# Second half of a projection: natural parts 512 columns wide between transposed parts, with four weight buffers lent by the attention's zone

## The chip, the core and the metric

The kernel runs on one core of one Trainium2 chip. A core has TensorE (matrix products into PSUM), VectorE (DVE), ScalarE (ACT), GpSimd (POOL), and SyncE (SP), whose queue issues the DMAs here. TensorE reads a stationary operand that a weight load (PEld) brings in, and streams a moving operand past it. Each engine executes its own instructions in the order in which the program gives them; semaphores hold one engine until another has finished what it needs.

The metric is the device time of one execution in microseconds. Before the change: median 1905.05 us of three runs (1902.53 to 1905.58).

## The reference

One layer of a streaming encoder. Every token is normalised, multiplied by one combined weight matrix, and its columns feed two branches: differential attention (q, k, v called qa, ka, va) and retention (qb, kb, vb). Each branch is gated (za, zb), projected, merged with two sigmoid gates (ga, gb), projected once more and added to the input.

```python
h = rmsnorm(x, norm_g) @ w_in                    # x: 2048 + 64 tokens x 1024, w_in: 1024 x 6144
qa, ka, va, za, qb, kb, vb, zb, ga, gb = split(h)  # eight parts of 512 columns, then two of 1024
qa, ka = rmsnorm per 64 columns(qa, ka)
a  = softmax(qa1 ka1) - lam * softmax(qa2 ka2)   # 4 heads, block-causal, distance bias
oa = a @ va
ob = retention(qb, kb, vb)                       # 4 heads, running state, blocks of 128 tokens
m  = sigmoid(ga) * ((rmsnorm(oa) * silu(za)) @ w_o_diff) + sigmoid(gb) * ((rmsnorm(ob) * silu(zb)) @ w_o_ret)
y  = x + m @ w_out
```

2048 prompt tokens run as one new stream; 64 sample tokens continue another one with 4096 cached keys and values. The normalised keys, the values and the retention states are outputs too.

## The kernel before

**Precision.** Operands are split into a high and a low part of the fast float format (`wh`, `wl` for weights, `xh`, `xl` for tokens), and each product is three matmuls: high by high, high by low, low by high (L998). A group over the whole inner dimension of 1024 has 8 chunks of 128, hence 24 matmuls.

**A planner orders the program.** The code is a set of Python generators, each a task with a priority. While the program is built, a planner keeps an estimated clock for each engine (`self.pe`, `self.act`, `self.dve`, `self.pool`, `self.dma`), with fixed costs for each instruction (`P`, `A`, `V`, `G`, `ld`, `st`, L204 to L241). A task yields the time or the condition it waits for; the ready task with the lowest priority number goes next (`loop`). Buffers are taken and given back by tag with such times (`take`, `give`). The order in which instructions are emitted is the order in which each engine executes them. The attention has priority 4 and its parts 0 to 3; the projection (`w_stream`) has 9, so it fills what the attention leaves free on TensorE.

**Projection in two halves of 1024 tokens.** The first half also carries the 64 sample tokens in its natural parts, and its transposed parts use a Strassen scheme (`strassen`). The second half does not. Its parts are of two kinds:

- *natural* (`natural`, L1092): 128 tokens are stationary and the weights' columns stream past, so the result has tokens on its partitions. Used for va, ka, qa and vb. With `wide` one 128-token tile makes 512 columns; without it two tiles of 256 columns share one PSUM bank, and the 512 columns of a part come as two calls. In the second half before, all natural parts are of the narrow kind.
- *transposed* (`transposed`, L1288): 128 columns of weights are stationary and tokens stream past in groups of 512, 256 and 320 (the last one with the 64 sample tokens). Used for qb, kb, za, zb, ga, gb in parts of 256 columns.

The second half before runs: va, ka, qa (first 256 columns each), mark `kqv0`; va, ka, qa (last 256 columns each), mark `kqv1`; vb twice; then qb, kb, mark `ret`, za, zb, ga, gb. The marks let the attention's heads 0 and 1, heads 2 and 3, and the retention of this half begin.

**Finishing a group.** PSUM has eight banks by tag: `mm` 2 (projection), `s` 2, `at` 2, `pv` 1, `tp` 1. A va tile leaves through a cast into `thi` (one buffer, L1246), a copy into `ev` (three buffers, L1248) and a difference into `tlo` (two, L1250); each buffer is free when its store to memory is done. ka and qa tiles square, sum, scale, are transposed on `tp` (L1202) and split. Transposed groups leave through `ev` alone (L1307 or L1309, then `put`).

**Weights.** A piece of weights is loaded into staging (`ws`, three buffers, L235 by way of `w_load`), ScalarE casts it into `wh` (L952) and GpSimd computes `wl` (L962). A wide piece is one chunk of 512 columns, a narrow one two chunks of 256; both take two buffers of the tag `w` (12 buffers), so a narrow part takes 8 in all and a wide one 16. In the first half four more, `wx`, stand in the pool of that half's zone. `w_room` (L631) and `w_pair` (L659) choose the buffers. A part keeps its pieces until its last group has read them.

**Attention's zone.** When the first half is over and the tokens of the second are split into high and low parts (`xt_ready`), `attn_zone` (L2676) frees the first half's zone and opens one for the attention: K and V of a head (four buffers each: two of each for a head of the first half, four of each in the second), q (two), and one long score area `row` of 12032 columns (`LATER`), an `Arena` from which contiguous spans are taken and given back piece by piece. For 128 queries and `nk` keys, `qk_block` (L1501) takes two rows of `nk` columns, `softmax` (L1544) exponentiates and combines them, and `at_pv` (L1589) transposes the combined row and multiplies it by V. Retention blocks take two spans of 1024 columns each from the same area, two blocks at a time, beside a table of 1024; its state takes 512.

`h_loader` and `q_loader` load K, V and q. For the very first head `load_head` (L1416) loads K, then q for the first two query pairs, the distance table `dfar`, then V, without a pause. `head_in` (L1464) lets the heads of a half begin 9 us (in the planner's clock) after their mark. When all attention and retention is done, the zone is closed and `out_prep` (L2198) loads the output weights and the first gated operands; `out_stream` begins when `w_stream` is over.

Of the kernel before, what the change touches and what calls it, by code (L numbers as in the profile page):

```python
# [49 lines left out]
LATER = 12032  # L50
# [38 lines left out]

class Arena:  # L90
    def __init__(self, tile, n):
        self.tile = tile
        self.at = [0.0] * (n // GRAIN)
        self.turn = 0

# [9 lines left out]
    def place(self, sizes, now):  # L105
# [18 lines left out]
        return [Span(self.tile[:, a * GRAIN:a * GRAIN + n], a, n) for (a, k, w), n in zip(got, sizes)], t  # L124
# [12 lines left out]
class Hybrid:  # L137
# [71 lines left out]
    def drop(self, span, t, lo=0, hi=None):  # L209
        self.ar.drop(span, t, lo, span.n if hi is None else hi)  # L210

# [419 lines left out]
    def w_room(self, wide, nw, q):  # L631

        if not wide:
            tags, pool, shape = ("w", "w"), self.wp, [128, 2, 256]
        elif nw in (0, 2):
            tags, pool, shape = ("S", "S"), self.ap, [128, 2, 512]
        else:
            tag, pool = yield from self.w_pair()
# [4 lines left out]
        elif u == 0:  # L643
            for tag in tags:
                yield from self.take(tag)
            self.wroom = [self.sb(pool, shape, tag, n, F32R) for tag, n in zip(tags, ("wh", "wl"))]
# [641 lines left out]
    def transposed(self, half, dst, d0, scale=None, grouped=True):  # L1288
        us = []
        groups = [(0, 0, 512), (1, 0, 256), (1, 256, 320)]  # L1290
        for ct in range(2):
            for k, (seg, col, n) in enumerate(groups):
                yield from self.take("mm")
                ps = self.psum("mm")[:, :n]
                last = ct == 1 and k == len(groups) - 1
# [112 lines left out]

    def attn_tables(self):
# [6 lines left out]
    def load_head(self, half, h):  # L1416
# [84 lines left out]
    def qk_block(self, h, p, b, ks, q, pair):  # L1501
# [6 lines left out]
        for c in range(2):  # L1508
            row = yield from self.grab(nk)
# [34 lines left out]
    def softmax(self, st, nk, b, pair):  # L1544
# [4 lines left out]
        half = nk if nk <= 1280 else (nk // 256) * 128  # L1549
# [26 lines left out]
        for sl in parts:  # L1576
# [5 lines left out]
            self.drop(rows[1], t2, sl.start, sl.stop)  # L1582
# [6 lines left out]
    def at_pv(self, h, p, vs, tv, pair, last_pair):  # L1589
# [27 lines left out]
        for kp in range(nkt // 2):  # L1617
# [15 lines left out]
            for row in arows:  # L1633
                self.drop(row, t, 256 * kp, min(256 * kp + 256, row.n))
# [963 lines left out]
    def w_stream(self):  # L2598
# [3 lines left out]
        fva = [(va + 256 * g, lambda half, g=g, f=f: self.natural(half, self.fin_va(g), f))  # L2602
               for g in range(2) for f in (True, False)]
        fva, fva0 = fva[1::2], fva[0]
        fk = [(ka + 256 * g, lambda half, g=g: self.natural(half, self.fin_qk("k", g))) for g in range(2)]
        fq = [(qa + 256 * g, lambda half, g=g: self.natural(half, self.fin_qk("q", g))) for g in range(2)]
        m0, m1 = (None, "kqv0"), (None, "kqv1")
        self.S, self.sunits, self.sraw, self.seg1_read, self.summed = {}, [], [], None, False
# [221 lines left out]
```

## Time and profile before

| quantity | value |
|---|---|
| median of three runs | 1905.05 us |
| the profiled execution, its own time | 1906.88 us |
| its span, first to last instruction | 1904.8 us |
| TensorE busy in the span | 1886.2 us, 99% |
| VectorE, ScalarE, GpSimd busy | 67%, 50%, 31% |
| granted clock, mean | 0.996 |
| second half's W work (natural from 584.0, transposed from 894.0, to the first output matmul) | 584.0 to 1545.5 us |

A matmul's listed duration includes the time it takes to run through the array, and matmuls overlap; the distance from start to start is what one costs when TensorE is full. Rows of busy time by stretches list, after the stretch and its length, busy us (and count) of PE, PEld, DVE, ACT and POOL, then the granted TensorE clock, the DMA engines' busy share and GB/s. Rows in order of time list start, duration, engine, line, operation, destination from source, count, and in brackets the idle time before and what ended it. Rows of waits list total us, times and the longest.

### The profile page before, as it was taken

Reading aid. Unit: us, or ns where it says so; the run is one execution under the profiler, and the core shown is the slowest. Engines: PE = TensorE matmul, PEld = TensorE weight load, DVE = VectorE, ACT = ScalarE, POOL = GpSimd, SP = SyncE. Lnnn points to the kernel's source line nnn. Section 1 sums busy time; section 2 is a strip of 40 time slices with the busy share of each in tenths; the row PEclk is TensorE's granted clock in tenths of the full one; section 3 lists DMA queues with packets and bytes.
Section 4 is the critical chain, followed back from the end, with each engine's and each line's share of the span. In section 5 each row is a group of like instructions: output and inputs, shape, how many; then the busy total and the mean of one; then the engine's idle time right before and its main releaser. Section 6 shows DMA issues by size and latency. Waiting matters only on the chain. (4 is left out here: it accounts for less than half of the span.)

```text
span 1904.8 us, 33589 instructions
## 1 busy us (share of the span) xinstructions
PE 1886.2 (99%) x11690; PEld 1691.2 (89%) x11690; DVE 1277.7 (67%) x3058; ACT 947.4 (50%) x2151; POOL 590.5 (31%) x557
## 2 busy tenths in 40 slices
PE   9999999999998999999999999999999999999999
PEld 7788888888887999999999989999999999999887
DVE  6765766657565787777676765676773139987664
ACT  6434554444443556565555565555565335554221
POOL 2420355556541212221111122111113515522442
PEclk9999999999998999999999999999999999999999
DMA  7654555565557848475325347435216548886542
GB/s 255 215 173 132 161 169 176 168 188 186 175 164 212 241 154 223 144 212 142 99 74 149 99 122 202 110 99 146 80 52 187 173 135 244 257 248 204 173 154 79
DMA packets 361323, 313.10 MB, mean 164 GB/s; under 512 B 67905, under 2 KB 319937, under 8 KB 361154
## 3 DMA queue, kind: packets, MB, share of 16 engines
q1 hardware_dynamic: 361154, 310.97, 55.7%
q8 instruction: 92, 1.51, 0.3%
q14 instruction: 77, 0.63, 0.1%
HBM read 205.43 MB, written 104.60 MB: 163 GB/s over the span
## 5 line engine op out<-in xcount | busy, mean ns | idle before, releaser
L962 POOL TENSOR_TENSOR wl<-ws,wh 128x512 fp32r<-128x512 f32 x125 | 171.9, 1389 | 373.5 <-ACT wh L952 326.1
L998 PE MATMUL mm<-xh,wh 128*128 128x512 f32 (+2 forms) x768 | 255.7, 333 | 0.0
L998 PE MATMUL mm<-xl,wh 128*128 128x512 f32 (+2 forms) x768 | 251.5, 327 | 0.0
L998 PE MATMUL mm<-xh,wl 128*128 128x512 f32 (+2 forms) x768 | 251.4, 327 | 0.0
L998 PE MATMUL mm<-wh,xh 128*128 128x256 f32 (+1 forms) x760 | 249.1, 328 | 0.0
L998 PE MATMUL mm<-wh,xl 128*128 128x256 f32 (+1 forms) x760 | 242.5, 319 | 0.0
L998 PE MATMUL mm<-wl,xh 128*128 128x256 f32 (+1 forms) x760 | 242.1, 319 | 0.0
L1644 DVE TENSOR_TENSOR atl<-at,ath 128x512 fp32r<-128x512 f32 (+1 forms) x144 | 93.6, 660 | 111.5 <-ACT ath L1642 110.9
L998 PEld LDWEIGHTS mm<-xh,wh 128*128 128x128 f32 x768 | 144.9, 189 | 11.1
L998 PEld LDWEIGHTS mm<-xl,wh 128*128 128x128 f32 x768 | 145.1, 189 | 10.7
L998 PEld LDWEIGHTS mm<-wh,xh 128*128 128x128 f32 x760 | 144.5, 190 | 11.2 <-DVE raw L1170 0.2
L998 PEld LDWEIGHTS mm<-wl,xh 128*128 128x128 f32 x760 | 144.5, 190 | 10.9
L998 PEld LDWEIGHTS mm<-xh,wl 128*128 128x128 f32 x768 | 144.8, 189 | 10.5
L998 PEld LDWEIGHTS mm<-wh,xl 128*128 128x128 f32 x760 | 144.3, 190 | 10.7
L1557 ACT ACTIVATE row<-row,a_mx 128x896 f32<-128x896 f32 (+5 forms) x144 | 149.3, 1040 | 8.1 <-DVE a_mx L1536 7.9
L1642 ACT CAST ath<-at 128x512 fp32r<-128x512 f32 (+1 forms) x144 | 79.8, 565 | 139.0 <-PE at L1629 138.1
L1399 POOL TENSOR_TENSOR r_y<-r_y,r_sq 128x256 f32<-128x256 f32 x32 | 30.2, 945 | 322.1 <-DVE r_sq L1396 129.6
L727 POOL TENSOR_TENSOR wl<-ws,wh 128x256 fp32r<-128x256 f32 x64 | 57.6, 899 | 193.8 <-ACT wh L718 188.7
L1526 DVE CUSTOM_DVE_ANT_0 row<-s,dfar 128x512 f32<-128x512 f32 (+2 forms) x147 | 90.5, 631 | 26.0 <-PE s L1518 25.4
L1517 PE MATMUL s<-K,q 128*128 128x512 f32 (+3 forms) x244 | 91.8, 378 | 8.1 <-DVE a_acc L1526 8.1
L1579 DVE SCALAR_TENSOR_TENSOR row<-row,a_w 128x896 f32<-128x896 f32 (+6 forms) x88 | 98.0, 1123 | 0.0
L1307 ACT COPY ev<-mm 128x512 f32<-128x512 f32 (+2 forms) x84 | 38.6, 460 | 113.2 <-PE mm L998 105.1
(497 smaller groups left out, 5489.7 us busy)
## 6 DMA issues: line engine op xcount, KB each, us to landing
ws<-in_w_in_dram SPq DMA_DIRECT2D x160, 256.0 KB, 3.2
q<-qT SPq DMA_DIRECT2D x128, 128.0 KB, 3.0
K<-kT SPq DMA_DIRECT2D x48, 256.0 KB, 5.2
V<-vN SPq DMA_DIRECT2D x24, 512.0 KB, 5.1
row<-in_x_prompt_dram SPq DMA_DIRECT2D x16, 512.0 KB, 4.4
wz<-in_w_in_dram SPq DMA_DIRECT2D x32, 256.0 KB, 4.5
row<-in_cache_k_T_dram SPq DMA_DIRECT2D x32, 256.0 KB, 3.6
row<-in_cache_v_diff_dram SPq DMA_DIRECT2D x32, 256.0 KB, 3.1
```

Of the source, the lines that this page charges most:

```text
L727: nc.gpsimd.tensor_sub(l[:, cs], src, h[:, cs].bitcast(F32))
L962: self.nc.gpsimd.tensor_sub(l, st, h.bitcast(F32))
L998: nc.tensor.matmul(ps, p, q, start=c == 0 and i == 0, stop=c == KC - 1 and i == 2)
L1307: nc.scalar.copy(ev, ps)
L1399: nc.gpsimd.tensor_mul(y, y, sq)
L1517: nc.tensor.matmul(ps, q1s, kk, start=True, stop=False)
L1526: nc.vector.tensor_tensor_reduce(out=row[:, k0:k0 + n], in0=ps, in1=tab, scale=-SLOPES[h], scalar=3.0e38, op0=ALU.add, op1=ALU.min, accum_ ...
L1557: nc.scalar.activation(u, u, AF.Exp, bias=mx, scale=-1.0, accum_out=lp[:, k:k + 1])
L1579: nc.vector.scalar_tensor_tensor(out=u0, in0=u1, scalar=w[:, 0:1], in1=u0, op0=ALU.mult, op1=ALU.add)
L1642: nc.scalar.copy(ah[:, :w], at[:, :w])
L1644: nc.vector.tensor_sub(al[:, :w], at[:, :w], ah[:, :w].bitcast(F32))
```

## The change

The second half's va, ka, qa and vb become wide parts (16 weight buffers each), and alternate with the first transposed parts: qb, va, qb, ka, kb, qa, marks `kqv0` and `kqv1`, kb, vb, mark `nat`, mark `ret`, za and the rest. The first transposed part of the half runs its token groups in another order, and each group waits for the tokens that it reads. Four W buffers (2048 columns) stand in the attention's zone in a pool `spare`; the score area shrinks from 12032 to 9984 columns, and once `nat` is done the pool is closed and its place is added to the area as a second tile. Rows of more than 1280 keys are taken as two spans of 1024 and the rest. The first head's loads are spread out in the planner's clock.

```diff
-LATER = 12032
+LATER = 9984
+MORE = 2048
+class Row:
+    def __init__(self, *spans):
+        self.spans = spans
+        self.n = sum(p.n for p in spans)
+
+    def piece(self, lo, hi):
+        for p in self.spans:
+            if hi <= p.n:
+                return p, lo, hi
+            lo, hi = lo - p.n, hi - p.n
...
 class Arena:
...
+    def add(self, tile, n, t):
+        self.tile.append((len(self.at) + 1, tile))
+        self.at += [None] + [t] * (n // GRAIN)
+        self.turn += 1
...
     def w_room(self, wide, nw, q):
         if not wide:
-            tags, pool, shape = ("w", "w"), self.wp, [128, 2, 256]
+            if any(p[0] for p in self.pieces):
+                tag, pool = yield from self.w_pair(4)
+            else:
+                yield from self.take("w", 2)
+                tag, pool = "w", self.wp
+            tags, shape = (tag, tag), [128, 2, 256]
...
-    def w_pair(self):
+    def w_pair(self, nw=0):
+        if nw >= 4 and not self.spare:
+            yield lambda: self.spare or len(self.res["w"].free) >= 2
+        if nw >= 4 and not self.spare:
+            yield from self.take("w", 2)
+            return "w", self.wp
         tag = yield from self.either(2, "w", "wx")
-        return tag, self.wp if tag == "w" else self.first
+        return tag, self.wp if tag == "w" else self.spare or self.first
...
     def transposed(self, half, dst, d0, scale=None, grouped=True):
         us = []
         groups = [(0, 0, 512), (1, 0, 256), (1, 256, 320)]
-        for ct in range(2):
-            for k, (seg, col, n) in enumerate(groups):
+        order = [(ct, k) for ct in range(2) for k in range(3)]
+        if self.npart[half] == 0:
+            groups = [(0, 0, 256), (0, 256, 256), (1, 0, 256), (1, 256, 320)]
+            order = [(0, 0), (1, 0), (0, 1), (1, 1), (0, 2), (0, 3), (1, 2), (1, 3)]
+        self.npart[half] += 1
+        for ct, k in order:
+                seg, col, n = groups[k]
+                need = min(8, (512 * seg + col + n) // 128)
+                yield lambda: len(self.xt_ready) >= need
+                yield max(self.xt_ready[:need])
                 yield from self.take("mm")
...
+    def more_rows(self):
+        yield lambda: "nat1" in self.done and len(self.res["wx"].free) == 4
+        yield max(self.res["wx"].free)
+        self.zs.close()
+        pool = self.z1.enter_context(self.tc.tile_pool(name="att2", bufs=1, side="right"))
+        self.ar.add(pool.tile([128, MORE], F32, tag="row2", name="row", bufs=1), MORE, self.pe)
...
         if not self.far:
             self.far = True
-            for p in range(2):
-                yield from self.load_q(0, p)
+            yield from self.load_q(0, 0)
+            yield self.pe + 3000
+            yield from self.load_q(0, 1)
+            yield self.pe + 2000
             self.ld(self.dfar, self.i["c_dfar"], 1 << 19)
...
-                yield lambda: self.far
+                yield lambda: len(self.heads) > 0 or h or half
...
-            row = yield from self.grab(nk)
+            row = Row(*(yield from self.grab(1024, nk - 1024))) if nk > 1280 else Row((yield from self.grab(nk)))
...
-        half = nk if nk <= 1280 else (nk // 256) * 128
+        half = nk if nk <= 1280 else 1024
...
-        later = [(vb + 256 * g, lambda half, g=g: self.natural(half, self.fin_vb(g, 2))) for g in range(2)]
+        wide = [(va, lambda half: self.natural(half, self.fin_va(0, 4), False, True), True),
+                (ka, lambda half: self.natural(half, self.fin_qk("k", 0, 4), False, True), True),
+                (qa, lambda half: self.natural(half, self.fin_qk("q", 0, 4), False, True), True)]
+        later = [(vb, lambda half: self.natural(half, self.fin_vb(), False, True), True)]
...
-        seqs = [first[0] + early + seq, first[1] + later + seq]
+        seqs = [first + early + seq, [seq[0], wide[0], seq[1], wide[1], seq[2], wide[2], m0, m1, seq[3], *later, (None, "nat"), *seq[4:]]]
...
         self.tp_ = self.z1.enter_context(self.tc.tile_pool(name="tmp", bufs=1, side="right"))
+        self.zs = ExitStack()
+        self.spare = self.zs.enter_context(self.tc.tile_pool(name="spare", bufs=1, side="right"))
+        self.res["wx"] = Res(4)
+        self.spawn(self.more_rows(), 0, "z")
         self.attn_tables()
```

More of the change, by code (lines that the diff above doesn't have):

```diff
@@ L637, in w_room @@
         else:
-            tag, pool = yield from self.w_pair()
+            tag, pool = yield from self.w_pair(nw)
             tags, shape = (tag, tag), [128, 1, 512]
@@ L643, in w_room @@
         elif u == 0:
-            for tag in tags:
-                yield from self.take(tag)
+            if wide:
+                yield from self.take("S", 2)
             self.wroom = [self.sb(pool, shape, tag, n, F32R) for tag, n in zip(tags, ("wh", "wl"))]
@@ L1581, in softmax @@
             t2 = self.V(n + 110, t)
-            self.drop(rows[1], t2, sl.start, sl.stop)
+            self.leave(rows[1], t2, sl.start, sl.stop)
             yield self.dve - PACE
@@ L2601, in w_stream @@
         gb = 5120
[L2602 to L2606, printed above, removed]
         m0, m1 = (None, "kqv0"), (None, "kqv1")
+        self.npart = [0, 0]
         self.S, self.sunits, self.sraw, self.seg1_read, self.summed = {}, [], [], None, False
```

24 lines of the change are left out of this document (16 added, 8 removed).

## The prediction

> **What bounds the kernel now.** First the page, for which engine fills the span; then busy time by stretches, for where TensorE does not fill it.
>
> ```profile
> span 1904.8 us, 33589 instructions
> PE 1886.2 (99%) x11690; PEld 1691.2 (89%) x11690; DVE 1277.7 (67%) x3058; ACT 947.4 (50%) x2151; POOL 590.5 (31%) x557
> 600.00:650.00 50.00, 42.14 (x316) 40.88 (x315) 28.84 (x103) 21.09 (x53) 7.23 (x6) 0.90 0.93 254
> 650.00:700.00 50.00, 50.00 (x417) 49.57 (x416) 38.73 (x120) 31.83 (x86) 11.76 (x9) 1.00 0.61 178
> 1550.00:1600.00 50.00, 48.02 (x383) 47.81 (x382) 41.57 (x85) 26.95 (x60) 22.96 (x22) 0.97 0.79 235
> ```
>
> TensorE is busy 1886.2 of 1904.8 us, so the time is the sum of its work plus 18.6 us in which it stands. Of those, 7.86 us lie in one stretch, 600 to 650, just where the second half begins and where the change works. PE's waits and its order of time there:
>
> ```profile
> PE s L1517 <- DVE a_acc L1526: 8.1, 2, 7.9
> 606.18 0.28 PE L998 MATMUL mm<-wh,xl 128*128 128x256 f32 x1
> 614.32 0.58 PE L1517 MATMUL s<-K,q 128*128 128x256 f32 x1 [7.86 <-DVE a_acc L1526]
> 614.91 0.41 PE L998 MATMUL mm<-wh,xh 128*128 128x256 f32 x1
> 615.13 0.41 PE L998 MATMUL mm<-wl,xh 128*128 128x256 f32 x1
> 619.16 0.29 PE L998 MATMUL mm<-wh,xh 128*128 128x256 f32 x1
> 610.00:615.00 5.00, 0.68 (x3) 0.68 (x4) 1.45 (x7) 2.29 (x6) 1.07 (x1) 0.50 0.97 318
> 615.00:620.00 5.00, 5.00 (x22) 4.64 (x22) 3.27 (x14) 3.62 (x12) 2.40 (x3) 0.59 0.70 207
> ```
>
> A score matmul waits for VectorE. The cause lies three engines back, in the rows of ScalarE, VectorE and the DMA queue:
>
> ```profile
> 612.26 0.59 ACT L1246 CAST thi<-mm 128x512 fp32r<-128x512 f32 x1 [15.41 <-DMA vN<-thi]
> 613.37 0.69 DVE L1250 TENSOR_TENSOR tlo<-mm,thi 128x512 fp32r<-128x512 f32 x1 [15.79 <-ACT raw L1248]
> 594.69 0.35 SPq L235 DMA_DIRECT2D dnear<-in_c_dnear_dram  x1
> 595.09 2.40 SPq L235 DMA_DIRECT2D K<-kT  x4
> 597.53 6.02 SPq L235 DMA_DIRECT2D q<-qT  x8
> 603.60 0.60 SPq L235 DMA_DIRECT2D dfar<-in_c_dfar_dram  x1
> 604.24 1.06 SPq L235 DMA_DIRECT2D V<-vN  x2
> 605.39 2.43 SPq L240 DMA_DIRECT2D vN<-thi  x1
> ```
>
> SP issues in order. The attention's first loads (dnear, four K, eight q, dfar, two V) keep it from 594.69 to 605.3; the store of `thi` behind them goes at 605.39. `thi` has one buffer, so the next cast into it starts at 612.26, VectorE stands behind that cast, and TensorE behind VectorE. After the gap the granted clock is 0.50 to 0.59 until 619.16: 256-wide matmuls step by 0.22 us (614.91, 615.13) where 0.12 is usual (below), so of the 4.84 us from 614.32 some 45% (2.1 us) are lost too. The stall costs **10.0 us**.
>
> **The change, part by part.**
>
> (1) Natural parts 512 wide. The work in matmul columns stays; the count halves.
>
> ```profile
> L998 PE MATMUL mm<-wh,xh 128*128 128x256 f32 x512 | 149.5, 292 | 0.0
> 584.02:594.81 10.79, 10.79 (x90) 10.79 (x90) 1.00 0.45 148
> 119.89 0.39 PE L998 MATMUL mm<-wh,xl 128*128 128x512 f32 x1
> 126.17 0.39 PE L998 MATMUL mm<-wh,xl 128*128 128x512 f32 x1
> 1500.10 0.39 PE L998 MATMUL mm<-xh,wh 128*128 128x512 f32 x1
> 1503.27 0.39 PE L998 MATMUL mm<-xh,wl 128*128 128x512 f32 x1
> ```
>
> Durations overlap (292 ns listed), so I price by start to start: 90 matmuls of 256 in 10.79 us are 0.1199 us each; from 119.89 to 126.17 there are 27 steps of 512, 0.2326 each; from 1500.10 to 1503.27, with the operands the other way round, 14 steps, 0.2264 each. Now 3 x 512 = 1536 matmuls of 256 (184.2 us) stand in the second half; then 768 of 512, 178.6 us by the second spacing, 173.9 by the third. Gain 5.5 to 10.3; I take **6**, near the row with the same operand order. All of it lies on the path, TensorE being full.
>
> The Trainium skill ("TensorE: Matmul & The Clock Gate", section "Back-to-back issue gap") gives a warm gap of N/2.4 + 2.5 ns, hence 109 and 216 ns; by it joining two matmuls saves 2.5 ns and all 768 pairs 1.9 us. The trace disagrees: 120 and 233.
>
> The first transposed unit takes four column groups for three: 48 matmuls of 512 become 96 of 256, 48 x (0.2398 - 0.2326) = +0.35 us. Casts, low parts, transposes and stores keep number and size (128x512 each); kT and qT are written in runs of 128 tokens for 256. Nothing on the path.
>
> (2) The burst under a transposed unit. That unit lasts 48 x (3 x 0.12 + 0.147) = 24.3 us (0.147 is the spacing of its 320-wide group, estimated from 0.12 and 0.23), 584 to 608, and leaves through `ev`, three buffers, with groups of 2.9 us: 8.6 us of cover, and 2.9 more in the second bank, against 5.76 for one `thi`. The burst is also cut: dnear, K and the first q are 9 issues (0.35 + 2.40 + 3.0 = 5.8 us of SP), then pauses of 3 and 2 us before the second q and dfar. A store of `ev` held 5.8 us at worst, and 6.9 more to landing (605.39 to 612.26 was that under load), is 12.7 against 11.5 us of cover: the stall shrinks to about nothing. Gain 0 to 10; I take **10**, since only an `ev` store issued right at the head of the burst meets both. If this cover is gone, the next one late is the cast into `ev`, and TensorE with it.
>
> (3) W supply. A wide part needs 16 buffers: beside a running narrow one (8 of 12) there is room for four of its eight pieces, two in the pool and two in the four new buffers. The rest wait for the narrow part's last group (3.5 us).
>
> ```profile
> ws<-in_w_in_dram SPq DMA_DIRECT2D x160, 256.0 KB, 3.2
> L952 ACT CAST wh<-ws x128: 602/621/665, 6.9 to 1520.0; 128x512 fp32r<-128x512 f32 x128
> L962 POOL TENSOR_TENSOR wl<-ws,wh x125: 1273/1297/2278, 7.6 to 1521.3; 128x512 fp32r<-128x512 f32 x125
> 1002.23 7.93 SPq L235 DMA_DIRECT2D K<-kT  x8
> ```
>
> Staging holds three pieces, so the eighth is loaded once the fifth is split: buffer free 2.6 us before the wide part, + 0.62 + 1.30, load 3.2, cast 0.62, low 1.30: ready 4.4 us after its start, needed after 7 x 3 x 0.2326 = 4.9. Margin half a microsecond at each of four starts; where it is missed, the planner runs attention if any is ready. Bounds: 0, and 8 us (one start behind a K burst of 7.93 on SP). I take **+2**, most starts lying where attention has work.
>
> (4) The rows shrink by 2048 columns until the vb part is done, and both marks for the second half's heads come after 3 narrow and 3 wide parts (72 + 134 = 206 us of W work) instead of after 67 us. Who waits for that:
>
> ```profile
> L998 PE MATMUL mm<-wh,xl x760: 278/283/415, 18.1 to 894.0; 128*128 128x256 f32 x128, 128*128 128x512 f32 x62
> 925.88 0.99 SPq L235 DMA_DIRECT2D V<-vN  x2
> 1435.79 0.89 SPq L235 DMA_DIRECT2D wst<-in_w_o_diff_dram  x2
> 1435.00:1505.00 70.00, 70.00 (x426) 64.18 (x426) 22.40 (x28) 33.90 (x64) 38.52 (x28) 1.00 0.75 218
> 1505.00:1545.00 40.00, 40.00 (x250) 37.12 (x250) 1.42 (x2) 6.76 (x14) 3.90 (x3) 1.00 0.25 72
> ```
>
> From 584 to 894 TensorE did 184 us of natural work, 10 of stall and so 116 of attention, retention and transposes. The marks fall at 584 + 206 + 116 = 906; with the planner's 9 us and eight K loads (7.93) the heads start near 925. They start there now: the last V buffers come at 925.88. Cost 0 (bounds: -5, rows in pieces being placed sooner, and +35 to the attention's end, if the narrow arena slows it as much as a whole pair's drain). It would not show at once either: the attention leaves at 1435.8, the output's preparation is done by about 1505 (VectorE 1.42 us busy after), and W work runs to 1545.
>
> **Sum**: 1904.8 - 6 - 10 + 0.35 + 2 = 1891.2 of span. The profiled execution took 1906.88, 2.1 outside the span; the median shown is 1905.05, so 13.65 less is **1891 us**.
>
> **Rivals.**
>
> A, the stall moves: with `ev` or, at about 614, the `thi` stores of the va part still behind q, dfar and V loads. For it: DMA share 0.97 there; against: of all the loads that natural tiles met in the second half, only this burst left a wait in PE's list. Part (2) gives 0 to 3: 1898 to 1901, say 1900.
>
> B, W pieces late at each start, 8 us instead of 2: 1897.
>
> C, the other side: attention late. Once W work ends at 1529 and the attention leaves after 1529 - 70 = 1459, 23 us later than now, TensorE runs out of filler and each further microsecond is paid whole. Slower than before needs 23 + 14 + 4 = 41 us. For it: 2048 of 12032 columns gone while retention holds 5120, late marks, heads that load K and V only between each other. Against: the gate today is V, not the marks. At 50 us late, 1891 + 27 = 1918.
>
> D, joining two matmuls into one saves next to nothing, 0 us for 6: 1897. The rows at 119.89 and 584.02 speak against it, since their spacing is that of long unbroken runs. The rule of the Trainium skill named above ("TensorE: Matmul & The Clock Gate", "Back-to-back issue gap") leans this way and would give 1895.
>
> **Chances and range.** Less than 0.2% (3.8 us) can't be told from no change. Forecast 0.55, A 0.17 (half of it inside 0.2%), B 0.07, D 0.02, C 0.19 (0.04 of it inside 0.2%). Faster 0.55 + 0.08 + 0.07 + 0.02 = 0.72; same 0.09 + 0.04 = 0.13; slower 0.15. The forecast's own range is 1884 (10.3 for 6, no W waits, part of 1550 to 1600's 2 us recovered) to 1897. The range asked for takes in A and the mild end of C: **1884 to 1907**.
>
> **What would show it.** Right: TensorE busy 50 of 50 and clock 1.00 from 600 to 650; 768 matmuls of 256 fewer in their place 768 of 512 on the natural line; the last natural or transposed matmul near 1530 instead of 1545. Wrong: a wait over 3 us on TensorE at the start of a wide part behind wl, or on the transposed part behind `ev`; first w_o load after 1459 and a gap between the W work's end and the first output matmul.

## The result, and the profile after

The changed kernel takes 1897.02 us (median of six runs, 1895.12 to 1898.76); the kernel before, run beside it, 1904.37 us (six runs, 1902.19 to 1905.58). The ratio is 0.9965, with a 95% interval of 0.9953 to 0.9977. The gain is 7.35 us, where the forecast had 13.65. The time lies in the range given; the size of the gain does not hold.

The page of the changed kernel first, and then its busy time by stretches (columns as before): 600 to 650, the W stage (the second half's W work up to the first output matmul), and the output.

```profile
span 1893.3 us, 32147 instructions
PE 1878.8 (99%) x10970; PEld 1651.3 (87%) x10970; DVE 1286.5 (68%) x3058; ACT 945.4 (50%) x2153; POOL 585.4 (31%) x557
```

```profile
600.00:650.00 50.00, 45.04 (x272) 40.30 (x271) 30.98 (x99) 24.25 (x62) 8.39 (x7) 0.97 0.96 258
583.80:1536.30 952.50, 946.68 (x6035) 859.75 (x6034) 633.64 (x1751) 517.42 (x1159) 190.93 (x154) 1.00 0.51 144
1536.30:1893.30 357.00, 351.05 (x2242) 318.03 (x2240) 267.09 (x466) 141.29 (x285) 135.94 (x103) 1.00 0.63 198
```

And the kernel before, in the same two stages:

```profile
583.80:1545.50 961.70, 953.14 (x6755) 898.45 (x6754) 629.93 (x1752) 519.84 (x1158) 196.91 (x154) 0.99 0.51 143
1545.50:1904.80 359.30, 352.39 (x2241) 319.66 (x2240) 262.15 (x465) 140.54 (x284) 135.22 (x102) 1.00 0.64 195
```

TensorE has 720 matmuls fewer (11690 to 10970): 768 fewer in the natural parts, and 48 more in the first transposed unit. The W stage got 9.2 us shorter, and it splits in two. Its idle time (length less busy time) went from 8.56 to 5.82 us. Busy time went down by 6.46 us, from 953.14 to 946.68. A part of the busy time is run at a lower clock. To take it out, I read the same view in stretches of 2 us and summed busy time x (1 - granted clock): 2.40 us before, 1.72 after. What is left is work at full clock: 950.7 us before, 944.9 after.

So in this pair of executions the width brought 5.8 us, and idle time and slow clock together fell by 10.96 - 7.54 = 3.4 us. From 600 to 650 TensorE is busy 45.04 of 50 us, not the 50 of 50 that the forecast named as the sign. TensorE's waits in the changed kernel (total us, times, longest), and then its order of time around three of them:

```profile
PE s L1574 <- DVE a_acc L1583: 2.5, 2, 2.3
PE at L2365 <- DVE ogl L2321: 2.3, 3, 0.9
PE s L2031 <- DMA row<-kbT: 1.0, 1, 1.0
PE s L1574 <- DMA q<-qT: 0.9, 1, 0.9
PE s L1575 <- DMA q<-qT: 0.7, 1, 0.7
```

```profile
604.17 0.30 PE L1574 MATMUL s<-K,q 128*128 128x128 f32 x1 [0.95 <-DMA q<-qT]
605.18 0.30 PE L1575 MATMUL s<-K,q 128*128 128x128 f32 x1 [0.71 <-DMA q<-qT]
607.00 0.42 PE L1038 MATMUL mm<-xl,wh 128*128 128x256 f32 x1
607.21 0.41 PE L1038 MATMUL mm<-xh,wl 128*128 128x256 f32 x1
623.25 1.21 SPq L265 DMA_DIRECT2D V<-vN  x2
624.56 5.09 SPq L265 DMA_DIRECT2D q<-qT  x4
629.75 0.54 SPq L270 DMA_DIRECT2D vN<-thi  x1
635.35 0.59 ACT L1286 CAST thi<-mm 128x512 fp32r<-128x512 f32 x1 [5.34 <-DMA vN<-thi]
636.46 0.69 DVE L1290 TENSOR_TENSOR tlo<-mm,thi 128x512 fp32r<-128x512 f32 x1 [5.10 <-ACT raw L1288]
639.00 0.50 PE L1574 MATMUL s<-K,q 128*128 128x512 f32 x1 [2.33 <-DVE a_acc L1583]
```

The chain that cost 7.86 us is there again, in small, 25 us later: two V and four q loads keep SP until 629.7, the store of `thi` stands behind them, the next cast into the one buffer waits 5.34 us, VectorE waits behind the cast, and TensorE 2.33 us behind VectorE. Ahead of it are two waits that were not there before: the first scores stand for q itself. After those, 256-wide matmuls step by 0.21 us (607.00, 607.21), the slow clock. The 7.54 us that are left in the stage are 2.33 behind the chain, 1.66 for q, 0.97 for a retention load (the third row of the waits), 1.72 of slow clock, and 0.86 outside 595 to 655.

A second profile of the same kernel (run e12) tells what belongs to the program and what to one execution.

### The profile page after: what moved, and what is told of

Its sections match the earlier page's. It is cut to its first block, busy times and chain, and to the rows that moved or that the text cites. A ratio compares the mean times of both kernels' runs of the same rounds, so it can differ in the third digit from the quotient of the medians.

```text
span 1893.3 us, 32147 instructions
## 1 busy us (share of the span) xinstructions
PE 1878.8 (99%) x10970; PEld 1651.3 (87%) x10970; DVE 1286.5 (68%) x3058; ACT 945.4 (50%) x2153; POOL 585.4 (31%) x557
## 4 chain that ended last, share of the span: by engine, by line
PE 64%; DVE 1%; DMA 1%; ACT 1%; issue 0%; SPq 0%; POOL 0%; DVEq 0%; ACTq 0%; POOLq 0%
PE mm L1038 28%; PE at L1686 3%; PE s L1575 3%; PE s L1574 3%; PE pv L1666 2%; PE pv L1665 2%; PE pv L1664 2%; PE s L2490 1%; PE s L2489 1%; PE s L2488 1%; PE at L2055 1%; PE mm L2489 1%; PE mm L2490 1%; PE at L2489 1%; PE at L2490 1%; PE at L2488 1%
## 5 line engine op out<-in xcount | busy, mean ns | idle before, releaser
L1038 PE MATMUL mm<-xh,wh 128*128 128x256 f32 (+2 forms) x784 | 259.9, 331 | 0.0
L1038 PE MATMUL mm<-xh,wl 128*128 128x256 f32 (+2 forms) x784 | 254.6, 325 | 0.0
L1038 PE MATMUL mm<-xl,wh 128*128 128x256 f32 (+2 forms) x784 | 254.6, 325 | 0.0
L1038 PE MATMUL mm<-wh,xh 128*128 128x512 f32 x504 | 203.2, 403 | 0.0
L1038 PE MATMUL mm<-wh,xl 128*128 128x512 f32 x504 | 197.8, 392 | 0.0
L1038 PE MATMUL mm<-wl,xh 128*128 128x512 f32 x504 | 197.5, 392 | 0.0
L1614 ACT ACTIVATE row<-row,a_mx 128x1024 f32<-128x1024 f32 (+7 forms) x144 | 149.8, 1042 | 13.5 <-DVE a_mx L1593 13.5
L1038 PEld LDWEIGHTS mm<-wh,xl 128*128 128x128 f32 x504 | 94.7, 188 | 21.3
L1038 PEld LDWEIGHTS mm<-wh,xh 128*128 128x128 f32 x504 | 94.8, 188 | 17.4 <-DVE raw L1210 0.2
L1636 DVE SCALAR_TENSOR_TENSOR row<-row,a_w 128x1024 f32<-128x1024 f32 (+5 forms) x88 | 97.0, 1108 | 0.0
```

The costliest lines, as they stand in the source:

```text
L1038: nc.tensor.matmul(ps, p, q, start=c == 0 and i == 0, stop=c == KC - 1 and i == 2)
L1614: nc.scalar.activation(u, u, AF.Exp, bias=mx, scale=-1.0, accum_out=lp[:, k:k + 1])
L1636: nc.vector.scalar_tensor_tensor(out=u0, in0=u1, scalar=w[:, 0:1], in1=u0, op0=ALU.mult, op1=ALU.add)
```

## The experiments

All ratios are to the kernel before, run on the same chip. The W stage's idle time is split at 595 to 655 us, where the attention begins; the last two columns are worked out as above, all in us. These four columns come from one profiled execution, which can differ from the median (by 4.3 us in e9 and 3.6 in e10), so a row need not add up. The medians of e2, e3, e5, e6, e8, e9, e11 and e15 lie outside the ranges of both theories that were set against each other, e5 alone on the fast side.

| kernel | median us | ratio (95%) | idle 595-655 | idle, rest of stage | lost to slow clock | work at full clock |
|---|---|---|---|---|---|---|
| before | 1904.37 | | 7.86 | 0.70 | 2.40 | 950.7 |
| after | 1897.02 | 0.9965 (0.9953-0.9977) | 4.96 | 0.86 | 1.72 | 944.9 |
| e1 before, two cast buffers | 1906.26 | 1.0012 (1.0004-1.0021) | 4.88 | 3.59 | 3.26 | 952.6 |
| e2 after, two cast buffers | 1905.07 | 1.0006 (0.9997-1.0014) | 4.80 | 5.70 | 4.83 | 946.2 |
| e3 after, matmuls cut | 1906.60 | 1.0014 (1.0005-1.0022) | 4.50 | 1.47 | 1.55 | 953.2 |
| e4 after, first scores 2 us later | 1897.00 | 0.9962 (0.9950-0.9973) | 6.31 | 2.41 | 1.71 | 946.0 |
| e5 after, long pauses | 1889.73 | 0.9925 (0.9913-0.9937) | 1.35 | 2.26 | 0.00 | 944.9 |
| e6 before, long pauses | 1906.21 | 1.0009 (1.0000-1.0018) | 3.16 | 6.71 | 2.89 | 953.3 |
| e7 after, no pauses | 1899.27 | 0.9976 (0.9965-0.9987) | 3.78 | 3.79 | 1.55 | 946.4 |
| e8 after, va first | 1910.81 | 1.0029 (1.0019-1.0040) | 6.55 | 7.54 | 3.18 | 947.4 |
| e9 long pauses, first head only | 1901.00 | 0.9980 (0.9969-0.9991) | 5.40 | 3.87 | 5.65 | 944.4 |
| e10 long pauses, the others only | 1897.30 | 0.9959 (0.9945-0.9974) | 2.30 | 5.10 | 1.69 | 947.3 |
| e11 after, landing counted longer | 1901.77 | 0.9988 (0.9978-0.9997) | 7.68 | 1.30 | 1.54 | 947.2 |
| e12 after, unchanged | 1897.58 (one run) | | 5.42 | 0.86 | 0.00 | 945.5 |
| e13 after, thi store on ScalarE's queue | 1897.65 | 0.9965 (0.9952-0.9978) | 6.30 | 0.83 | 0.00 | 946.2 |
| e14 before, the same | 1900.64 | 0.9980 (0.9971-0.9990) | 4.02 | 1.28 | 1.70 | 951.5 |
| e15 after, q loads on GpSimd's queue | 1899.21 | 0.9970 (0.9960-0.9981) | 5.15 | 0.88 | 2.88 | 944.7 |
| e16 e5 and thi store aside | 1890.77 | 0.9928 (0.9914-0.9943) | 1.30 | 2.46 | 1.70 | 944.9 |
| e17 long pauses a little other | 1901.00 | 0.9979 (0.9969-0.9989) | 1.72 | 6.04 | 3.22 | 945.8 |

**The one cast buffer (e1, e2).** A second buffer `thx` beside `thi`, taken from the score area, opened with the attention's zone (e1's edit; in e2 `LATER` goes from 9984 to 9472):

```diff
-LATER = 12032
+LATER = 11520
...
-            yield from self.take("thi")
+            hit = yield from self.either(1, "thi", "thx")
```

> The kernel before, with a second buffer for the high-part cast of the va, ka and qa tiles, in the attention's zone (512 score columns fewer: 11520). Theory: the stall of 7.86 us at 606 to 614 is the single cast buffer whose store stands behind the first loads on SP. With two, the third tile takes the buffer that was stored before the burst, and only the fourth can meet it: TensorE's wait there falls from 7.86 to 0 to 3 us, the slow clock behind it goes or halves, and the time is 7 to 10 us below before: 1895 to 1898. Rival (ev or tlo stores behind the same burst hold the tile as long): the wait stays over 5 us and the time above 1900.

> The changed kernel with the same second cast buffer (score area 9472 for 9984). Theory: the wait of 2.33 us at 639 is again the one cast buffer behind V and q loads (store issued at 629.75, 6 us late); it goes, the rest stays: 1.5 to 2.5 us below the changed kernel, about 1895. Rival (the late attention, with fewer score columns still later, is what keeps the gain away): no gain or a loss, 1897 to 1900, and the attention leaves later than the 1465 of the changed kernel.

The wait named by the profile went, and the time did not get shorter. In the kernel before, TensorE now stands for the q loads of the same burst:

```profile
608.05 0.41 PE L1519 MATMUL s<-K,q 128*128 128x384 f32 x1 [0.35 <-DMA q<-qT]
619.03 0.35 PE L1518 MATMUL tp<-K,q 128*128 128x256 f32 x1 [3.91 <-DMA q<-qT]
620.01 0.55 PE L1519 MATMUL tp<-K,q 128*128 128x256 f32 x1 [0.62 <-DMA q<-qT]
```

In the changed kernel the 2.33 us went as well, and waits of 1.40 us at 605.85 (q), 2.10 at 931.84 and 2.35 at 1048.05 (both behind VectorE) came up, and the retention's wait near 646 grew from 0.97 to 2.03 us. So the one buffer belongs to the chain of the named wait, but the expected gains (7 to 10 us in e1, 1.5 to 2.5 in e2) did not come. The attention did leave later in e2, as its rival had it (first output weights loaded at 1475.28, 1464.93 in the changed kernel), but the time was lost earlier: idle time and slow clock of the stage are 15.3 us for 7.5. The edit changes the planner's order too, so it left open how much of the 10 us is to be had without that; e14 answers this.

**The width (e3).** Each 512-wide natural matmul of the second half becomes two of 256, at the same place and with the planner's costs unchanged. The two halves' sums in one bank aren't kept apart; the work on TensorE is that of two halves.

```diff
...
-nc.tensor.matmul(ps, p, q, start=c == 0 and i == 0, stop=c == KC - 1 and i == 2)
+for u in (slice(0, 256), slice(256, 512)):
+    nc.tensor.matmul(ps[:, u], p, q[:, u], start=c == 0 and i == 0, stop=c == KC - 1 and i == 2, ...)
```

> The changed kernel with each 512-wide natural matmul of the second half issued as two of 256, in the same place and with the planner's costs unchanged, so that order, buffers and loads are those of the changed kernel. Theory: the width is worth 768 x (2 x 0.1199 - 0.2326) = 5.5 us, 6 as forecast: 1902 to 1903.5. Rival (width is worth a fixed 2.5 ns a pair, and the gain seen comes from the stall): 1 to 2 us, 1898 to 1899.

The whole gain is gone, 9.6 us over the changed kernel; work rises by 8.3 us. Over all the kernels here, those with narrow natural parts (before, e1, e3, e6, e14) have 952.3 us of work on the mean, the wide ones (all others but e8, where va is narrow) 945.7: a difference of 6.6. The step holds, with a price between 5.8 and 8.3.

**Order and moment (e4, e7, e8).** e4 lets the planner place the first two pairs' scores 2 us later; e7 takes out the two pauses; e8 puts va first, in two narrow calls, as the kernel before has it.

```diff
-            yield tq
+            yield tq + (2000 if half == h == 0 and p < 2 else 0)
...
-            yield self.pe + 3000
-            yield self.pe + 2000
...
-[seq[0], wide[0], seq[1], wide[1], seq[2], wide[2], m0, m1,
+[*nva, seq[0], wide[1], seq[1], wide[2], seq[2], m0, m1,
```

> The changed kernel, where the planner puts the first two query pairs' score matmuls 2 us later behind the landing of q. Theory: TensorE's waits of 0.95 and 0.71 us for q at 604 and the slow clock of about 1.5 us behind them come from a landing that the planner's estimate has too early; both go and the time falls by 2 to 3 us: 1894 to 1895. Rival (in that stretch the DMA queue is the bound, whatever the order): the waits move to the next q or to V, and the time stays within 1 us of 1897.

> The changed kernel without its two pauses: both q, the distance table and V follow K at once, as before the change, but under the transposed part. Prediction's theory (the transposed part with its three evacuation buffers covers the burst by itself): within 2 us of the changed kernel, 1896 to 1899. New theory (queue's load): waits of q, V and of the stores behind them grow by 2 to 5 us: 1899 to 1902.

> The changed kernel with va first again, as two narrow parts of 256 columns before the first transposed part (so va alone is narrow: 192 pairs of matmuls, 1.4 us more), ka, qa, vb wide as changed, the pauses kept. Prediction's theory (the burst must not lie under va's one cast buffer): the stall of about 8 us and its slow clock come back: 1904 to 1908. New theory (the queue's load decides, not the kind of part): waits as in the changed kernel within 3 us: 1897 to 1901.

In e4 the waits at 604 and 605 turned into later ones, the longest of 2.47 us at 616.63, again for q, and the time is the same. Without the pauses it is 2 us more, but the intervals of e7 and the changed kernel overlap and the stretch stands less, not more (3.78 us for 4.96), so a worth of the two pauses is not shown. With va first it is slower than before: 14.1 us idle, half of it outside the stretch. The expected stall of 8 us did not come back, though: the longest wait of the stretch is 2.10 us, again for q, beside 1.34 behind VectorE. So this order is worse than the changed kernel's, and how much of that is due to the kind of part over the burst is not shown.

**Loads further apart (e5, e6, e9, e10).** e5 makes all the pauses longer; e6 brings the pauses, as long as in e5, and the changed kernel's condition for the later q loads into the kernel before; e9 has only those of the first head, e10 only the other two.

```diff
             yield from self.load_q(0, 0)
-            yield self.pe + 3000
+            yield self.pe + 8000
             yield from self.load_q(0, 1)
-            yield self.pe + 2000
+            yield self.pe + 6000
             self.ld(self.dfar, self.i["c_dfar"], 1 << 19)
+            yield self.pe + 4000
...
-                yield self.pe + CALM
+                yield self.pe + 24000
...
-        yield self.pe + 2 * CALM
+        yield self.pe + 64000
```

> The changed kernel with the attention's first loads further apart: pauses of 8, 6 and 4 us after the first q, the second q and the distance table (3, 2 and 0 in the changed kernel), the second head's loads 24 us after (18), retention 64 us after the mark (36). Nothing is taken away. Theory (new): the waits of the W stage between 600 and 650 come from more loads than the DMA queue carries in that time, whichever buffer is hit; spread out, TensorE does W work instead. Idle and slow-clock time of the W stage falls from 7.5 to 2 to 4 us: 1892 to 1894. Rival (each wait is a miss of the planner's estimate, and a new order only draws new ones): the waits stay at 5 to 10 us in other places, 1895 to 1900.

> The kernel before, order and width as they were, with the spread of loads of the run e5. Theory (the queue's load is what stalls): the 7.86 us wait at 606 to 614 goes and most of the slow clock with it, 1896 to 1899, without the change's order. Rival (only a unit that needs no cast buffer covers the burst, as the prediction had it): a wait of 4 us or more remains, 1900 to 1905.

> The changed kernel with only the pauses among the very first head's loads lengthened (8, 6 and 4 us instead of 3, 2 and 0), the second head's loads and the retention's start as in the changed kernel. Theory (transfer load of 595 to 655 us spoils what the transposed part covers): most of the 7.4 us that all the lengthened pauses together gained over the changed kernel comes from here, 1891 to 1893, with no wait over 1.5 us in 595 to 640 and at most the retention's wait near 647 left. Rival (each new order draws its own waits, the gain of the lengthened pauses was a lucky draw): no trend, 1895 to 1900, with new waits of 1 to 2.5 us elsewhere.

> The changed kernel with only the second head's loads (24 us after the first head's instead of 18) and the retention's start (64 us instead of 36) put later, the first head's pauses as in the changed kernel. Theory: the waits at 604, 605 and 639 us (0.95, 0.71 and 2.33 us) stay, as they belong to the first head's loads; the 0.97 us of the retention's load near 647 goes: 1895 to 1897. Rival (lucky draw): anything from 1890 to 1900, the waits at 604 to 639 changed as well.

e5 beats both kernels: 1889.73 us. The stretch by the same view, first in the changed kernel and then in e5:

```profile
595.00:655.00 60.00, 55.04 (x344) 49.79 (x343) 34.65 (x108) 30.68 (x77) 10.94 (x9) 0.97 0.94 254
595.00:655.00 60.00, 58.65 (x341) 51.64 (x340) 27.80 (x94) 27.37 (x66) 9.75 (x8) 1.00 0.96 262
```

TensorE is busy 58.65 of 60 us there at a clock of 1.00 (55.04 at 0.97 in the changed kernel). The stretch did not carry fewer transfers, however: the DMA engines' share is 0.96 and the rate 262 GB/s, for 0.94 and 254. What changed is which loads go when, and what is placed between them; the theory of a lighter queue is not borne out by these rows. And neither half of the edit gained anything alone. In e9 the delayed loads of the first head run into those of the second, in order of time:

```profile
637.12 0.59 ACT L1286 CAST thi<-mm 128x512 fp32r<-128x512 f32 x1 [0.59 <-PE mm L1038]
638.24 10.29 SPq L265 DMA_DIRECT2D q<-qT  x8
648.62 0.54 SPq L270 DMA_DIRECT2D vN<-thi  x1
651.97 0.59 ACT L1286 CAST thi<-mm 128x512 fp32r<-128x512 f32 x1 [6.36 <-DMA vN<-thi]
654.41 1.12 PE L1687 MATMUL at<-ident,row 128*128 128x128 f32 x4 [3.63 <-DVE row L2073]
```

It is the forecast's chain once more: eight q loads keep SP 10.29 us, and the store of the `thi` written at 637.12 goes at 648.62. A retention load at 1084.28 costs e9 another 3.38 us. In e10 the wait at 639 went, against the expectation, while 1.22 and 0.50 us for q stayed at 605 and 606; the stretch is better (2.30 us idle), and 5.10 us stand elsewhere. And e6 did nothing for the kernel before: the stretch got better there too (3.16 us idle for 7.86), but 6.71 us of waits came up elsewhere, 2.70 of them at 732.76 for a retention load.

**The estimate (e11).** The planner counts 2.5 us more for each landing in the first 70 us after the zone opens.

```diff
-        return self.dma + DMA_LAT
+        return self.dma + DMA_LAT + (2500 if self.pe < self.busy else 0)
```

> The changed kernel, whose planner counts 2.5 us more for the landing of every load in the first 70 us of its clock after the attention's zone opens; nothing is loaded later on purpose, only the users of loaded data are placed later. Theory (the load itself spoils it): the q waits near 604 to 620 shrink under 0.5 us, but the wait of the score matmul for VectorE behind the thi store (2.33 us at 639) stays or moves, as that store stands in SP's queue behind the same loads: 1894 to 1896. Rival (only the planner's fixed estimate is wrong): nearly all waits of 595 to 655 go, 1890 to 1892, as with the lengthened pauses.

Slower by 4.7 us than the changed kernel. The q waits shrank to 0.6 us and less, about as expected, but a wait of 4.70 us came at 647.90, on ScalarE's `ath`; putting only the users later doesn't help.

**The same kernel again (e12).**

> The changed kernel itself, profiled a second time. Theory: the waits of 595 to 655 us stand at the same instructions, each within 0.7 us of the first profile's (0.95, 0.71, 2.33, 0.97), 4 to 6 us in all; waits of the output stage (0.9 and smaller ones) differ more, since nothing in the order fixes them. Rival (the waits are noise of one execution): other instructions wait, or the total of 595 to 655 is under 2 us.

```profile
603.87 0.30 PE L1574 MATMUL s<-K,q 128*128 128x128 f32 x1 [0.95 <-DMA q<-qT]
604.93 0.30 PE L1575 MATMUL s<-K,q 128*128 128x128 f32 x1 [0.77 <-DMA q<-qT]
638.69 0.50 PE L1574 MATMUL s<-K,q 128*128 128x512 f32 x1 [2.20 <-DVE a_acc L1583]
1615.30 0.39 PE L2365 MATMUL at<-ogl,w_o_diffh 128*128 128x264 f32 x1 [2.33 <-DVE ogl L2321]
```

The waits of the stretch belong to the program: the same instructions stand, 0.95, 0.77 and 2.20 us for 0.95, 0.71 and 2.33, and 5.42 us in all for 4.96. Two more waits for q (0.52 and 0.59) stand beside them, and the retention's 0.97 is 0.40. The output stage does not repeat: 360.5 us for 357.0, with a wait of 2.33 us at 1615 whose longest was 0.9 in the first profile.

**SP's queue or the transfers (e13, e14, e15).** These keep the planner's order. e13 and e14 issue the `thi` stores of the second half's va tiles from ScalarE's queue, in the changed kernel and in the one before; e15 issues the first head's q loads from GpSimd's.

```diff
     def st(self, dst, src, nbytes=0):
-        self.nc.sync.dma_start(dst, src)
+        (self.nc.scalar if self.aside else self.nc.sync).dma_start(dst, src)
...
     def ld(self, dst, src, nbytes=0):
-        self.nc.sync.dma_start(dst, src)
+        (self.nc.gpsimd if self.aside else self.nc.sync).dma_start(dst, src)
```

> The changed kernel with one edit: in the second half the store of thi goes by ScalarE's queue, right behind the cast, and no longer by SP's. The planner's order is the same. Theory (SP's queue order made the 2.33 us at 639): the first thi store goes near 624 instead of 629.75, the next cast stands under 1 us behind it instead of 5.34, the 2.33 us are gone, the q waits at 604 and 605 stay: 1894 to 1895.5. Rival (the transfers are late, not their issue): the store goes at 624 but lands near 634 all the same, the wait stays over 1 us: 1896.5 to 1898.

> The kernel before with the same edit, the order of the planner being the same: the stall of 7.86 us at 606.5 and the slow clock behind it (2.1 us), which the forecast held to be worth 10 us. Theory (SP's queue order): the first thi store goes near 598 instead of 605.39, the 7.86 us shrink under 2, the slow clock with it; what is left are q waits of 1 to 4 us at 608 to 620 as with the two cast buffers: 1899 to 1902. Rival (the waits only change place): under 2 us gained, 1903 to 1905.

> The changed kernel with one edit: the q loads of the first head (first half's four pairs) go by GpSimd's queue instead of SP's; the planner's order is the same. Theory (SP's queue order): SP no longer stands 5.09 us at 624.56, so the thi store goes near 625 and the 2.33 us at 639 are gone; the q waits at 604 and 605 change by what GpSimd's issue costs: 1893 to 1896. Rival (the transfers are the limit): the same waits within 0.7 us, 1896.5 to 1898.5.

e14 is the forecast's step by itself, in the kernel it was made for. Its order of time:

```profile
597.54 0.42 ACTq L241 DMA_DIRECT2D vN<-thi  x1
598.72 8.51 SPq L236 DMA_DIRECT2D q<-qT  x8
604.10 0.59 ACT L1247 CAST thi<-mm 128x512 fp32r<-128x512 f32 x1 [6.11 <-DMA vN<-thi]
610.91 0.41 PE L1521 MATMUL s<-K,q 128*128 128x384 f32 x1 [1.59 <-DMA q<-qT]
621.09 0.35 PE L1520 MATMUL tp<-K,q 128*128 128x256 f32 x1 [1.58 <-DMA q<-qT]
```

ScalarE sends the store at 597.54, while the q loads keep SP until 607.2 (in the kernel before it went at 605.39). The next cast stands at 604.10 instead of 612.26, and the wait of 7.86 us is gone without trace. The gain is 3.9 us of median (1904.55 to 1900.64; 3.96 by idle time and slow clock). The rest went to q waits (3.88 us in all) and the slow clock after them. In the kernel before, TensorE's waits have none for q: the stall had covered them. Part of these waits may be new, since SP needs 8.51 us for the eight q loads here, and 6.02 before. In e13 the same edit gains nothing. The store goes 5.2 us earlier than in the changed kernel, and the next cast still waits for its landing, but only 3.2 us earlier than there:

```profile
624.50 0.35 ACTq L271 DMA_DIRECT2D vN<-thi  x1
632.14 0.59 ACT L1287 CAST thi<-mm 128x512 fp32r<-128x512 f32 x1 [2.40 <-DMA vN<-thi]
635.94 0.41 PE L1577 MATMUL s<-K,q 128*128 128x384 f32 x1 [1.38 <-DMA q<-qT]
```

The 2.33 us at 639 are gone, and waits for q (1.38 and 0.30 at 636) and of retention's matmuls (1.21 and 0.92 at 645 and 648) stand in their place. In e15 the wait at 639 is gone and so are all later ones of the stretch but one of 0.81 us, but q comes later still, with a wait of 3.27 us at 607.67. Whether the later waits went for SP's free queue or for the 4.3 us that TensorE had stood by then, this run does not tell. Taking one of these waits away hands its time to the next.

**Is e5 a rule or a draw? (e16, e17)** e16 is e5 with the va tiles' `thi` stores on ScalarE's queue; e17 changes three of e5's pauses a little (9.5 for 8, 26 for 24, 68 for 64 us).

> The kernel with all the longer pauses (e5, 1889.73), with the thi stores of the second half on ScalarE's queue; the same order. Theory (with the loads spread, SP's queue holds no store long enough to matter): the q waits at 621 and 622 stay, 1888.5 to 1891. Rival: new waits as in e13, 1892 to 1895.

> The changed kernel with long pauses a little other than e5's (9.5, 6 and 4 us among the first head's loads, second head after 26 us, retention after 68). Theory (a lighter stretch of transfers gains): within 2 us of e5, 1888 to 1892, waits of 595 to 700 us under 3 us in all. Rival (e5 was one good draw among orders): 1894 to 1901, with a wait over 1.5 us between 595 and 700.

The stretch obeys: 1.30 and 1.72 us idle, as in e5 (1.35). The total of e16, whose order is e5's, does so too (1890.77 us); that of e17 does not (1901.00). In e17 the planner's other order drew two waits far from the burst, which e5 lacks:

```profile
810.08 1.11 PE L1242 MATMUL tp<-ident,raw 128*128 128x128 f32 x4 [2.37 <-DVE tlo L1258]
934.37 0.63 PE L1242 MATMUL tp<-ident,raw 128*128 128x128 f32 x4 [2.10 <-DVE raw L1227]
```

So all pauses together cleared 595 to 655 in both orders of the changed kernel that were tried; that e5 also stayed clean elsewhere is, by e17, a property of that one order.

## Why the prediction was off in size

**The step that failed** is part (2): "the stall shrinks to about nothing. Gain 0 to 10; I take **10**". It measured 3.4 us (10.96 us of idle time and slow clock in the stage, 7.54 after; 4.7 by the second profile, which shows 6.28). The chain was read rightly: e14 takes away only the store's place on SP, and the 7.86 us go. What failed is the price, and with it the claim that nothing would be left. I took a stall that the profile names as time to be had whole. Under it lay the next limit, the q loads of the same burst: e14 shows that the store's place is worth 3.9 us in the kernel before, and e1 shows the same q waits with a second buffer. In the changed kernel the cover asked for was that of `ev` alone, and the chain of `thi` came back behind a later group of loads (2.33 us). The forecast named the cast into `ev` as the next one late, and did not ask when the loads themselves land for the scores that were placed by a fixed estimate (1.66 us for q, and a slow clock behind it).

Rival A (the stall moves, 0 to 3 us of gain for this part, 1900) was the nearer one. Its mechanism came in its second form, `thi` stores of va behind q and V loads, at 629.75 and not at 614; its price of 0 to 3 for 3.4 was about right. It did not name the q waits either. In the changed kernel no wait of TensorE leads back to `ev`.

**Part (1)**, the width, forecast 6 less 0.35, is 5.8 us in the profiled pair and 6.6 over all kernels: right. By the rule of the Trainium skill ("TensorE: Matmul & The Clock Gate", "Back-to-back issue gap"), worked out with the prediction, it would have been an estimated 1.9 us; the runs disagree, and rival D falls. That section of the Trainium skill gives the formula for a single isolated matmul, and about 131 ns at 512 columns for a stream of weight loads and matmuls; the prediction's steps of 0.2264 and 0.2326 us at 512 columns disagree with that figure too.

**Part (3)**, forecast +2, is 0: no wait for `wl` in the second half of the changed kernel. Where such waits do stand (0.6 to 1.7 us between 1496 and 1528 in e4, e7, e8, e10 and e11) they belong to the last transposed parts and not to the start of a wide one. Rival B falls.

**Part (4)**: cost 0 came out, but one of its two reasons failed. The forecast had the second half's heads start near 925, as in the kernel before ("the gate today is V, not the marks"). Before, their first score matmul stands at 926.46; in the changed kernel it stands 24 us later, and the attention left 29 us later (1464.93 for 1435.79), past rival C's point of 1459. The rows of before, of the changed kernel (two) and of e9:

```profile
926.46 0.39 PE L1517 MATMUL s<-K,q 128*128 128x512 f32 x1
950.34 0.39 PE L1574 MATMUL s<-K,q 128*128 128x512 f32 x1
1464.93 1.23 SPq L265 DMA_DIRECT2D wst<-in_w_o_diff_dram  x1
1487.56 0.90 SPq L265 DMA_DIRECT2D wst<-in_w_o_diff_dram  x2
```

No gap opened, and the output stage took no longer, since the other reason, the slack, held. W work ran to 1536.3, so the point had moved to 1536 - 70 = 1466, about a microsecond after the attention left; with W work ending at 1529, as forecast, the attention would have been 6 us past it. But the 70 us were too cautious: in e9 the first output weights are loaded at 1487.56, 59 us before the first output matmul at 1546.5, which does not wait, and its output stage takes 356.8 us. So rival C's late attention came in both runs, and its gap in neither. (The 67 us of the forecast for three narrow calls are 69 by its own 0.1199 us a matmul; nothing else rests on them.)

**The sum.** By the stage, -5.8 and -3.4 make -9.2, and the output stage of this pair another -2.3; by the medians it is -7.35. The profiled execution of before was 2.5 us above its median and that of after 1.9 below, and e12's output stage was 3.5 us longer than the first profile's. The output stage's 2.3 us are therefore not put down to the change. If the width is worth 5.8 to 6.6 us, the medians leave only 0.8 to 1.5 us for all the rest, so the 3.4 us of part (2) are more likely its upper end. Which part of before's 10.96 us stands in its median execution was not tried.

## What to carry to other kernels

In this case a stall that the profile names was an upper bound of what its removal brought (3.4 and 3.9 us for 10, and a loss in e1, whose order changed too): before it is priced whole, look at everything that was due in its shadow, above all transfers of the same burst whose users were placed by an estimate. Where a planner fixes the order, a new order draws its own small waits (here 0.7 to 7.5 us outside the stretch that was worked on), so an edit is judged by the stage it was meant for and by the total, and an edit that keeps the planner's order (another queue for one store) tells more than one that does not. Work done with fewer and wider matmuls came through every order tried (944.4 to 947.3 us at full clock, for 950.7 to 953.3).

## What the runs showed of the hardware

The cost of issuing on SP was in places larger than I had reckoned (3.0 us for four q loads of 128 KB). In the changed kernel four of them keep SP 2.54 us in a quiet stretch (DMA share 0.34 from 771 to 775) and 5.09 us at 624.56 (DMA share 1.11 there); eight of them take 10.29 us in e9. Four others, at 598.06, took 2.56 us at a share of 1.05, so the share alone does not set it. The row of the quiet stretch:

```profile
771.72 2.54 SPq L265 DMA_DIRECT2D q<-qT  x4
```

The changed kernel's DMA view (issues, KB each, median us from issue to landing), for 595 to 655 us and for the whole run:

```profile
q<-qT SPq DMA_DIRECT2D x20, 128.0 KB, 5.0
q<-qT SPq DMA_DIRECT2D x128, 128.0 KB, 3.1
```

The median q load takes 5.0 us to land in the stretch, and 3.1 us in the whole run. The Trainium skill ("DMA: Bandwidth & Descriptors", section "Issuing engines are not separate DMA queues") says that issuing from several engines saves only the sequencer's time, usually small beside the transfer. For one load this holds here: 5.09 us for four is 1.27 us of issue each, beside 5.0 us to landing. But a store behind four or eight loads waits for the sum of their issues, and e14 gained 3.9 us by sending it from another queue. In e13 the early store took 7.6 us to land where the late one of the changed kernel took 5.5, which agrees with one set of DMA engines behind both queues; e13 and e15 gained nothing.

The clock can fall after short waits: in the changed kernel two waits of 0.95 and 0.71 us, which began 1.3 us apart, were followed by steps of 0.21 us for 256 columns, and 1.72 us were lost. In e12 almost the same two waits (0.95 and 0.77) cost no slow clock in the stage at all.
